# A convolution and pooling trunk on one core: modulation columns taken in twos, the layer norm's scaling in product order, and one pair of products halved around the mean

## The chip, the cores and the metric

One core of a Trainium2 chip runs the whole kernel in one launch. The metric is device time in microseconds (us): the median of several executions of the kernel. A single execution is also recorded by the hardware profiler; its rows are what is read here as "the profile" and "the trace". TensorE (PE) does the matmuls, and PEld is its weight load, which runs beside them. VectorE (DVE), ScalarE (ACT) and GpSimd (POOL) do the elementwise work, and SyncE (SP) issues most of the DMAs from memory.

## What is computed

```python
D_MODEL = 1024; SEQ = 1024; DEPTH = 2; CONV_WIDTH = 31; D_FF = 2816

def conformer_conv(h, w1, b1, w_dw, b_dw, ln_g, ln_b, w2, b2):
    u = h @ w1 + b1
    a, g = jnp.split(u, 2, axis=-1)
    u = a * jax.nn.sigmoid(g)
    u = causal_depthwise_conv(u, w_dw) + b_dw          # 31 taps
    u = jax.nn.silu(layer_norm(u, ln_g, ln_b))
    return u @ w2 + b2
...
c_act = jax.nn.silu(c)
for i in range(DEPTH):
    mod = c_act @ ada_w[i] + ada_b[i]
    sh_m, sc_m, g_m, sh_f, sc_f, g_f = jnp.split(mod, 6, axis=-1)
    h = modulate(rms_norm(x, norm_mix_g[i]), sh_m, sc_m)
    y = conformer_conv(h, ...) if i % 2 == 0 else multiscale_pool(h, ...)
    x = x + (1.0 + g_m)[:, None, :] * y
    h = modulate(rms_norm(x, norm_ffn_g[i]), sh_f, sc_f)
    y = (jax.nn.silu(h @ w_gate) * (h @ w_up)) @ w_down
    x = x + (1.0 + g_f)[:, None, :] * y
return rms_norm(x, final_g)
```

The inputs are float32. The six parts of `mod` (numbered j = 0 to 5) depend on the conditioning vector `c` alone. Here only layer 0 matters, the one with the convolution.

## The kernel before

**Tiling.** The 1024 positions are two chunks of 512, A and B. Channels lie on the 128 partitions, so an activation of a chunk is eight tiles (k = 0 to 7) of 128 x 512. Every weight and every activation of a large product is split into a high and a low part (`whi`, `wlo`, `hhi`, `hlo`, `vhi`, `vlo`), and `products` (L414) makes three matmuls of 512 columns of them, high by high, low by high and high by low, for each of the eight k. So one output tile of 128 channels takes 24 matmuls. All matmuls are recorded at one line (L128), and all elementwise operations at one line (L106), so in the rows one goes by tile names.

**Order.** The order of PE's instructions is that in which the program writes them. The other engines' queues are ordered by a scheduler from what each instruction depends on. Around the main products the program steps through `Task`s, generators that write side work. `pace` is called in the loops over `products` and steps them by a model clock: a task says `yield "load"`, and is not stepped again until the model clock has moved by the number that `LOAD` gives for that word. `finish` steps a task to its end at once. A chain of dependencies can be added by hand (`tc.add_manual_dep`).

**Layer 0.** Conv pairs: for each p of 8, `conv_in` makes an `a` tile and a `g` tile (24 products each) and `conv_glu` turns them into `u`, with a sigmoid on ACT and a multiply on DVE. The taps of the depthwise convolution run on DVE, ACT and POOL. A's pairs come first, then B's, with A's layer norm (`layer_norm_silu`) beside B's pairs. That norm sums the eight filtered tiles on DVE (`acc`), has PE form the mean (`mean`), subtracts, squares, has PE form the variance (`var`, one column for each 128 positions), computes a reciprocal root in a dozen small DVE steps, and has PE spread it over the partitions (`rstd`). Then each tile is scaled by `rstd` on DVE, passes through silu on ACT, and is split into `vhi` and `vlo`. The scheduler chooses the order of these scalings and splits. `conv_out` multiplies the eight tiles by the second weight (`y`, 8 output tiles, 192 products), ACT evicts (`t<-y`), and DVE adds to `x`. Squares of the new `x` give the next norm (`norm_a`, again a `var` and a `rstd`) behind which the first FFN's `gate` products start.

**Modulation columns.** Parts j = 0 and 1 are computed at the start of the kernel. Parts 2 to 5 come from `ada_columns` (L358) as a `Task` beside the conv pairs. For each j and each k it loads a tile `adaw` of 512 KB (128 x 1024, `ada_load`, L138, on SP's queue) and makes four matmuls of 256 columns (`ada`, counted x8 in the trace). That is 32 column steps. `adaw` has `ADA_BUFS` = 2 buffers. A load is written when the column two before it has been written, so it waits for that column on PE. After the eighth k of a j, `columns_done` copies the row off PSUM on ACT (`t<-ada`), turns it into columns by two small matmuls (`adac`), and adds the bias. When the flag `held` is set (before the last of B's pairs), the parts j = 3 to 5 that end after it keep their row in `held_back`, and `conv_out` writes their `columns_done` in its second step. `finish(T["ada", 0])` forces what columns are left.

**Weights.** `load_weight` loads a raw tile on SP, copies its high part on ACT, and makes the low part either by a subtraction or, with `summed`, by a negated copy on ACT followed by an accumulating DMA on POOL's queue (L408).

**End of this stretch.** The units are written in this order: B's pairs but the last, `held`, the finish of the columns, the finish of A's taps, B's last pair but for those `HOLD` = 1 holds, `need("ln_a")`, `conv_out(A)`, the task `norm_a`, the held pair, `need("norm_a")`, and then the first FFN.

Of the kernel before, what the change touches and what calls it, by code (L numbers as in the profile page):

```python
# [19 lines left out]
KT = D // P  # L20
# [26 lines left out]
PHTAPS = 29  # L47
PHLEN = 135
OUT_B = 3
LOAD = {"load": 2.5, "slow": 18.0, "next": 4.0}  # L50
AHEAD = 4
STRETCH = 1.35
LATER = 300
# [58 lines left out]
def trunk(ctx, tc, xT, c, vec, ada, adan, w1, w2, wgu, wdn, wpl, wph, out):  # L112
# [37 lines left out]
    def either(n):  # L150

        now = clock["PE"]
        v, g = (max(clock[e], now) + engines[e].price("tensor_tensor", n) for e in "VG")
        return V_ if v <= g else G_
# [29 lines left out]
    def pace(ahead=AHEAD):  # L184

        for t in [t for t in tasks if t.urgent or getattr(t, "free", False)]:
            while step(t, "V"):
                pass
        moved = True
        while moved and tasks:  # L190
            moved = False
            for e in "VG":
                if clock[e] < clock["PE"] + ahead:
                    moved = any(step(t, e) for t in list(tasks)) or moved
# [41 lines left out]
    def slot(ch, name, dt=F32R):  # L236

        return slots.tile([P, ch.n], dt, tag=f"s{ch.i}", name=nm(name))
# [5 lines left out]
    def bank(name):  # L244
        return ps.tile([P, 512], F32, tag="mm", name=nm(name))

    def spare_bank(name):

        return ps.tile([P, 512], F32, tag="ca", name=nm(name), bufs=2)
# [11 lines left out]
    def temp(n, name="t", bufs=0):  # L261
        t = tmp.tile([P, TMPW], F32, tag=name if bufs else "t", name=nm(name), bufs=bufs or 4)
        return t[:, :n]
# [47 lines left out]
    def ada_load(src):  # L311
        w = raws.tile([P, D], F32, tag="ada", name=nm("adaw"), bufs=ADA_BUFS)
        sync.dma_start(w, src)
        return w
# [43 lines left out]
    def ada_columns(js):  # L358


        todo = [(j, k) for j in js for k in range(KT)]
        src = lambda j, k: adan[k, :, (j - 2) * D : (j - 1) * D]
        ws = [ada_load(src(*t)) for t in todo[:ADA_BUFS]]
        for i, (j, k) in enumerate(todo):
            yield "load"
            if k == 0:
                acc = bank("ada")
            w = ws.pop(0)
            for g in range(4):
                matmul(acc[32 * g : 32 * g + 32, :Q], ccols[:, k, :], w[:, g * Q : g * Q + Q], start=k == 0, stop=k == KT - 1)  # L370
            clock["PE"] -= 1.3
            if i + ADA_BUFS < len(todo):
                ws.append(ada_load(src(*todo[i + ADA_BUFS])))
            if k == KT - 1 and (j == 2 or not held[0]):
                yield from columns_done(j, acc)
            elif k == KT - 1:
                held_back.append((j, acc))
# [36 lines left out]
    def products(out, wt, k, act, first, last, o=0, n=None):  # L414

        wk = slice(k * P, (k + 1) * P)
        for i, (wp, a) in enumerate(((0, 0), (0, 1), (1, 0))):
            cols = act[a][:, o : o + n] if n else act[a]
            matmul(out, wt[wp][:, wk], cols, start=first and i == 0, stop=last and i == 2)
# [149 lines left out]
    def conv_u(ch, p):  # L569
        u = st["u", ch.i, p] = wslot(ch, "u")  # L570
        if ch.i == 0:
            G_.memset(u[:, :HALO], 0.0)
        else:
            G_.tensor_copy(u[:, :HALO], uhalo[:, p, :])
        return u
# [9 lines left out]
    def conv_in(*todo):  # L585

        def emit(take):
            got = {}
            for each in todo:
                if each is None:  # L590
                    finish(T["norm_b"])
                    continue
                if callable(each):
                    each()
                    continue
                ch, p = each
                conv_u(ch, p)
                wts = got.setdefault(p, [])
                b = [bank("a"), bank("g")]
                for i in range(2):  # L600
                    if len(wts) == i:
                        wts.append(take())
                    for k in range(KT):
                        products(b[i], wts[i], k, st["h", ch.i][k], k == 0, k == KT - 1)
                        if k % 4 == 3:
                            pace()
                conv_glu(ch, p, *b)
                if ch.i == 0 and p not in PHASED:
                    T["taps", 0, p] = Taps(A, p)
        tiles = list(dict.fromkeys(e[1] for e in todo if isinstance(e, tuple)))  # L610
        unit(emit, *[w1[p, i] for p in tiles for i in range(2)])

    class Taps:


# [110 lines left out]
    def centred(vs, mean, n):  # L726
# [7 lines left out]
                V_.tensor_tensor(vs[k], vs[k], mean, op=SUB)  # L734
        yield

    def layer_norm_silu(ch):

        n = ch.n
        vs = [st["u", ch.i, k][:, HALO:] for k in range(KT)]  # L740
        acc = temp(n, "acc", 2)
        for k in range(1, KT):
            while not (st["taps", ch.i][k - 1] and st["taps", ch.i][k]):
                yield "wait"
            V_.tensor_tensor(acc, vs[0] if k == 1 else acc, vs[k], op=ADD)
            yield
        yield "stats"
        b = bank("mean")
        matmul(b, ones, acc, start=True, stop=True)
        if ch.i == 0:  # L750
            yield from centred(vs, b, n)
        else:
            for k in range(KT):
                V_.tensor_tensor(vs[k], vs[k], b, op=SUB)
                yield
        acc = yield from sum_sq([vs[k] for k in CENTRED], n)
        rstd = yield from mean_rsqrt(acc, n)
        S_.activation(tmp.tile([P, 16], F32, tag="col0", name=nm("col"), bufs=1)[:, 0:1], acc[:, 0:1], AF.Silu)
        hv = [(slot(ch, "vhi"), slot(ch, "vlo")) for _ in range(KT)]
        for k in range(KT):  # L760
            V_.tensor_tensor(vs[k], vs[k], rstd, op=MUL)
            sw = temp(n)
            S_.activation(sw, vs[k], AF.Silu, bias=V("conv_ln_b", k), scale=V("conv_ln_g", k))
            hi, lo = hv[k]
            if ch.i == 0 and k % 2 == 0:
                V_.tensor_copy(hi, sw)
            else:
                S_.copy(hi, sw)
            (either(n) if ch.i else (G_, V_)[k % 2]).tensor_tensor(lo, sw, hi.bitcast(F32), op=SUB)
            yield  # L770
        st["v", ch.i] = hv

# [517 lines left out]
    def need(*names):  # L1290
        unit(lambda take: finish(*(T[n] for n in names)))
# [44 lines left out]
    unit(lambda take: finish(*(T["taps", 0, p] for p in range(KT) if p not in PHASED)))  # L1336
    for p in rest[len(rest) - HOLD - HOLD_LN : len(rest) - HOLD]:
        conv_in((B, p))
    need("ln_a")
    sq_a = Squares(A)  # L1340
    conv_out(A, sq_a, lambda take: [now(columns_done(*g)) for g in held_back])
    unit(lambda take: T.__setitem__("norm_a", Task(norm(A, 0, True, ("h", 0), squares=sq_a), True)))
    for p in rest[len(rest) - HOLD :]:
        conv_in((B, p))
    need("norm_a")
    unit(lambda take: stretch.__setitem__(0, STRETCH))

# [135 lines left out]
```

## Time and profile before

| | us |
|---|---|
| median of 3 runs | 1840.85 (1838.78 to 1842.66) |
| profiled execution | 1842.04 |
| its span | 1840.2 |
| PE busy | 1777.9 (97%) |
| DVE busy | 1312.9 (71%) |
| ACT busy | 1040.9 (57%) |
| POOL busy | 588.4 (32%) |

The profiled execution's time is 1.8 us longer than the span of its instructions and 1.2 us above the median. Times of rows are counted from the span's start. In the rows of a view "[1.86 <-DMA x]" says that the engine stood idle for 1.86 us ahead and what ended the wait. Shares of busy time are averages over stages with different limits, so the change has to be read in the stretch that it touches: the conv layer of chunk A, up to about 323 us.

### The profile page before, as it was taken

Reading aid. Unit: us, or ns where it says so; the run is one execution under the profiler, and the core shown is the slowest. Engines: PE = TensorE matmul, PEld = TensorE weight load, DVE = VectorE, ACT = ScalarE, POOL = GpSimd, SP = SyncE. Lnnn points to the kernel's source line nnn. Section 1 sums busy time; section 2 is a strip of 40 time slices with the busy share of each in tenths; the row PEclk is TensorE's granted clock in tenths of the full one; section 3 lists DMA queues with packets and bytes.
Section 4 is the critical chain, followed back from the end, with each engine's and each line's share of the span. In section 5 each row is a group of like instructions: output and inputs, shape, how many; then the busy total and the mean of one; then the engine's idle time right before and its main releaser. Section 6 shows DMA issues by size and latency. Waiting matters only on the chain.

```text
span 1840.2 us, 26108 instructions
## 1 busy us (share of the span) xinstructions
PE 1777.9 (97%) x9672; PEld 1514.0 (82%) x9672; DVE 1312.9 (71%) x2125; ACT 1040.9 (57%) x1610; POOL 588.4 (32%) x628
## 2 busy tenths in 40 slices
PE   6999989999999999999999999999999999999996
PEld 4766677888888887889997888999988789999985
DVE  7789855988875238779978448778684468887735
ACT  3656666776647455555546456555564546555543
POOL 3479732877833111311116121111151211011111
PEclk9999999999999999999999999999999999999998
DMA  7978858888888987867766887655568866655562
GB/s 253 298 221 239 218 130 202 213 230 206 230 208 210 234 222 179 242 192 202 206 178 150 199 181 171 163 137 136 147 143 210 187 151 170 182 139 138 127 138 69
DMA packets 115953, 342.73 MB, mean 186 GB/s; under 512 B 11505, under 2 KB 21873, under 8 KB 115826
## 3 DMA queue, kind: packets, MB, share of 16 engines
q1 hardware_dynamic: 76944, 223.60, 36.7%
q0 software_dynamic: 37728, 116.41, 35.2%
q8 instruction: 76, 1.25, 0.3%
q10 hardware_dynamic: 1154, 1.05, 0.2%
q14 instruction: 51, 0.42, 0.1%
HBM read 336.83 MB, written 4.19 MB: 185 GB/s over the span
## 4 chain that ended last, share of the span: by engine, by line
PE 82%; DMA 6%; DVE 6%; ACT 2%; issue 2%; POOL 1%; SPq 0%; DVEq 0%; ACTq 0%; POOLq 0%
PE dn L128 22%; PE gate L128 22%; PE up L128 22%; PE y L128 6%; PE a L128 3%; PE g L128 3%; PE first L128 2%; DMA adaw<-in_adan_dram 2%; DMA raw<-in_wgu_dram 2%; DMA w<-in_wdn_dram 1%; DVE x L106 1%; DVE t L106 1%; DMA w<-in_wgu_dram 1%; ACT w L106 1%; PE ada L128 1%
## 5 line engine op out<-in xcount | busy, mean ns | idle before, releaser
L128 PE MATMUL dn<-ghi,w 128*128 128x512 f32 (+1 forms) x1440 | 470.0, 389 | 4.1 <-DMA w<-in_wdn_dram 2.7
L106 ACT ACTIVATE w<-raw 128x1024 fp32r<-128x1024 f32 (+1 forms) x262 | 243.0, 927 | 326.1 <-PE dn L128 99.0
L106 ACT CAST w<-raw 128x512 fp32r<-128x512 f32 (+1 forms) x392 | 322.1, 824 | 144.9 <-PE up L128 53.5
L106 DVE SCALAR_TENSOR_TENSOR x<-dn,gains,x 128x512 f32<-128x512 f32 (+1 forms) x360 | 263.3, 736 | 83.2 <-PE dn L128 80.4
L128 PE MATMUL gate<-hhi,w 128*128 128x512 f32 (+1 forms) x1088 | 313.0, 361 | 4.2 <-DMA w<-in_wgu_dram 3.9
L128 PEld LDWEIGHTS dn<-ghi,w 128*128 128x128 f32 x1440 | 269.1, 188 | 57.8 <-DMA w<-in_wdn_dram 3.6
L128 PE MATMUL up<-hhi,w 128*128 128x512 f32 (+1 forms) x1088 | 310.1, 358 | 0.0
L128 PE MATMUL dn<-glo,w 128*128 128x512 f32 (+1 forms) x720 | 279.2, 388 | 0.9 <-POOL glo L106 0.9
L106 POOL TENSOR_TENSOR pa<-pa,pr 128x512 f32<-128x512 f32 x168 | 229.7, 1419 | 22.5 <-ACT pr L106 19.5
L128 PEld LDWEIGHTS gate<-hhi,w 128*128 128x128 f32 x1088 | 198.2, 190 | 36.6 <-DMA w<-in_wgu_dram 4.7
L1008 POOL DMA_DIRECT2D w<-in_wgu_dram x80 | 69.6, 871 | 495.8 <-ACT w L106 161.7
L128 PEld LDWEIGHTS up<-hhi,w 128*128 128x128 f32 x1088 | 196.6, 189 | 30.5
L128 PE MATMUL gate<-hlo,w 128*128 128x512 f32 (+1 forms) x544 | 196.1, 361 | 1.5 <-DVE hlo L106 1.5
L128 PE MATMUL up<-hlo,w 128*128 128x512 f32 (+1 forms) x544 | 194.6, 358 | 0.0
L408 POOL DMA_DIRECT2D w<-in_wgu_dram x96 | 86.2, 898 | 324.8 <-ACT w L106 301.1
L106 DVE TENSOR_TENSOR t<-t,up 128x512 f32<-128x512 f32 (+1 forms) x88 | 55.0, 625 | 169.3 <-PE up L128 156.6
L106 DVE SCALAR_TENSOR_TENSOR ca<-u,vecs,ca 128x512 f32<-128x512 f32 x252 | 174.1, 749 | 0.7
L128 PEld LDWEIGHTS dn<-glo,w 128*128 128x128 f32 x720 | 136.2, 189 | 24.0 <-POOL glo L106 1.2
L106 ACT ACTIVATE pr<-u,vecs 128x512 f32<-128x512 f32 x168 | 113.3, 715 | 16.7 <-POOL pa L106 6.9
L128 PEld LDWEIGHTS gate<-hlo,w 128*128 128x128 f32 x544 | 103.7, 191 | 18.2 <-DVE hlo L106 2.3
L128 PEld LDWEIGHTS up<-hlo,w 128*128 128x128 f32 x544 | 102.7, 189 | 15.5
L106 DVE TENSOR_TENSOR w<-raw,w 128x512 fp32r<-128x512 f32 (+1 forms) x122 | 84.4, 700 | 31.0 <-ACT w L106 27.9
(188 smaller groups left out, 3385.5 us busy)
## 6 DMA issues: line engine op xcount, KB each, us to landing
raw<-in_wgu_dram SPq DMA_DIRECT2D x176, 512.0 KB, 5.2
w<-in_wgu_dram POOLq DMA_DIRECT2D x96, 512.0 KB, 8.2
raw<-in_wdn_dram SPq DMA_DIRECT2D x88, 512.0 KB, 5.5
adaw<-in_ada_dram SPq DMA_DIRECT2D x64, 512.0 KB, 5.8
w<-in_wdn_dram POOLq DMA_DIRECT2D x48, 512.0 KB, 8.3
raw<-in_w_dram SPq DMA_DIRECT2D x44, 512.0 KB, 6.0
w<-in_wgu_dram POOLq DMA_DIRECT2D x80, 256.0 KB, 5.4
w<-in_w_dram POOLq DMA_DIRECT2D x34, 512.0 KB, 8.3
```

What stands on the lines that cost most here:

```text
L106: self.last = self.order(getattr(self.eng, name)(out, *args, **kw))
L128: last_mm[0] = nc.tensor.matmul(out, lhsT, rhs, start=start, stop=stop, **kw).ins.name
L408: order(nc.gpsimd.dma_start(as_src(lo), src, accum_op=ADD))
L1008: order(nc.gpsimd.dma_start(lo, src, accum_op=ADD))
```

## The change

It has three parts.

1. The columns are taken in twos. `ada_columns` yields "load" ahead of every second column only, with 7.0 on the model clock instead of 2.5, and "late" (14.0) ahead of the first. The loads are issued in twos when a pair is written, instead of one for each column.
2. The scaling, silu and splits of chunk A's layer norm are written by `silu_in_order`. It chains DVE's multiplies, casts and subtractions by hand in the order in which the products take the tiles, with the multiply two tiles ahead. The even tiles' high part is cast on DVE and the odd ones' on ACT. The odd tiles and tile 0 are subtracted on DVE and the other even ones on POOL. (Before, DVE subtracted the odd tiles, and POOL all even ones.)
3. `conv_halves` splits B's held pair. Its `a` half is written ahead of `need("ln_a")`. Its `g` half and the `conv_glu` stay behind `conv_out`.

```diff
-LOAD = {"load": 2.5, "slow": 18.0, "next": 4.0}
+LOAD = {"load": 7.0, "late": 14.0, "slow": 18.0, "next": 4.0}
...
         for i, (j, k) in enumerate(todo):
-            yield "load"
+            if i % ADA_BUFS == 0:
+                yield "load" if i else "late"
...
-            if i + ADA_BUFS < len(todo):
-                ws.append(ada_load(src(*todo[i + ADA_BUFS])))
+            if i % ADA_BUFS == ADA_BUFS - 1:
+                ws += [ada_load(src(*t)) for t in todo[i + 1 : i + 1 + ADA_BUFS]]
...
+    def conv_halves(ch, p):
+        got = {}
+        def first(take):
+            conv_u(ch, p)
+            got["a"] = spare_bank("a")
+            wt = take()
+            for k in range(KT):
+                products(got["a"], wt, k, st["h", ch.i][k], k == 0, k == KT - 1)
+                if k % 2:
+                    pace()
+        def second(take):
+            b, wt = bank("g"), take()
+            for k in range(KT):
+                products(b, wt, k, st["h", ch.i][k], k == 0, k == KT - 1)
+                if k % 2:
+                    pace()
+            conv_glu(ch, p, got["a"], b)
+        return (first, w1[p, 0]), (second, w1[p, 1])
...
+    def silu_in_order(vs, rstd, hv, n):
+        last = [None]
+        def chained():
+            if last[0] is not None:
+                tc.add_manual_dep(V_.last.ins, last[0], edge, reason="as the products take them")
+            last[0] = V_.last.ins.name
+        def scaled(k):
+            V_.tensor_tensor(vs[k], vs[k], rstd, op=MUL)
+            chained()
+            sw = temp(n)
+            S_.activation(sw, vs[k], AF.Silu, bias=V("conv_ln_b", k), scale=V("conv_ln_g", k))
+            return sw
+        ahead = [scaled(0), scaled(1)]
+        for k in range(KT):
+            sw = ahead.pop(0)
+            hi, lo = hv[k]
+            if k % 2 == 0:
+                V_.tensor_copy(hi, sw)
+                chained()
+            else:
+                S_.copy(hi, sw)
+            if k % 2 or k == 0:
+                V_.tensor_tensor(lo, sw, hi.bitcast(F32), op=SUB)
+                chained()
+            else:
+                G_.tensor_tensor(lo, sw, hi.bitcast(F32), op=SUB)
+            if k + 2 < KT:
+                ahead.append(scaled(k + 2))
+            yield
...
         hv = [(slot(ch, "vhi"), slot(ch, "vlo")) for _ in range(KT)]
+        if ch.i == 0:
+            yield from silu_in_order(vs, rstd, hv, n)
+            st["v", ch.i] = hv
+            return
         for k in range(KT):
...
             hi, lo = hv[k]
-            if ch.i == 0 and k % 2 == 0:
-                V_.tensor_copy(hi, sw)
-            else:
-                S_.copy(hi, sw)
-            (either(n) if ch.i else (G_, V_)[k % 2]).tensor_tensor(lo, sw, hi.bitcast(F32), op=SUB)
+            S_.copy(hi, sw)
+            either(n).tensor_tensor(lo, sw, hi.bitcast(F32), op=SUB)
...
+    held_a, held_g = conv_halves(B, rest[-1])
+    unit(*held_a)
     need("ln_a")
     sq_a = Squares(A)
     conv_out(A, sq_a, lambda take: [now(columns_done(*g)) for g in held_back])
     unit(lambda take: T.__setitem__("norm_a", Task(norm(A, 0, True, ("h", 0), squares=sq_a), True)))
-    for p in rest[len(rest) - HOLD :]:
-        conv_in((B, p))
+    unit(*held_g)
     need("norm_a")
```

What this does to the queues is seen at four places. In the rows a name is "out<-inputs" with the number of the buffer, and x4 or x2 says how many instructions a row stands for.

First, PE's queue around chunk A's `rstd`. Before, the last `g` products of the pair ahead stand in front of it (its `var` stands 13 rows higher), and the `y` products right behind:

```order
L128 MATMUL g_2127<-hhi_718,w_2016 128x512
L128 MATMUL g_2127<-hlo_719,w_2016 128x512
L128 MATMUL g_2127<-hhi_718,w_2017 128x512
L128 MATMUL rstd_2201<-ident,col_2177 128x128 x4
L128 MATMUL y_2281<-vhi_2208,w_2119 128x512
L128 MATMUL y_2281<-vlo_2209,w_2119 128x512
```

Now the same `rstd` has `var` and eight columns right in front, and the `a` products of the held half behind it:

```order
L128 MATMUL var_2131<-ones,acc_2033 128x1 x4
L128 MATMUL ada_2149<-adaw_2015,ccols 32x256 x4
L128 MATMUL ada_2149<-adaw_2017,ccols 32x256 x4
L128 MATMUL ada_2149<-adaw_2158,ccols 32x256 x4
L128 MATMUL ada_2149<-adaw_2160,ccols 32x256 x4
L128 MATMUL ada_2149<-adaw_2187,ccols 32x256 x4
L128 MATMUL ada_2149<-adaw_2189,ccols 32x256 x4
L128 MATMUL ada_2149<-adaw_2199,ccols 32x256 x4
L128 MATMUL ada_2149<-adaw_2201,ccols 32x256 x4
L128 MATMUL rstd_2211<-ident,col_2137 128x128 x4
L128 MATMUL a_2276<-hhi_688,w_2046 128x512
L128 MATMUL a_2276<-hlo_689,w_2046 128x512
```

The last eight columns (all of j = 5) moved from among the products to between `var` and `rstd`, and 24 `a` products moved between `rstd` and the first `y`.

Second, SP's queue of loads at that place. Before, column loads and the raw weight tiles alternate, and the columns end before `raw_2267`:

```order
L138 DMA adaw_1826<-in_adan_dram 128x1024
L138 DMA adaw_1855<-in_adan_dram 128x1024
L403 DMA raw_2128<-in_w_dram 128x1024
L138 DMA adaw_1910<-in_adan_dram 128x1024
L138 DMA adaw_1929<-in_adan_dram 128x1024
L403 DMA raw_2267<-in_w_dram 128x1024
L403 DMA raw_2274<-in_w_dram 128x1024
L403 DMA raw_2342<-in_w_dram 128x1024
```

Now the last six column loads stand in a row:

```order
L138 DMA adaw_2017<-in_adan_dram 128x1024
L404 DMA raw_2383<-in_w_dram 128x1024
L404 DMA raw_2421<-in_w_dram 128x1024
L138 DMA adaw_2158<-in_adan_dram 128x1024
L138 DMA adaw_2160<-in_adan_dram 128x1024
L138 DMA adaw_2187<-in_adan_dram 128x1024
L138 DMA adaw_2189<-in_adan_dram 128x1024
L138 DMA adaw_2199<-in_adan_dram 128x1024
L138 DMA adaw_2201<-in_adan_dram 128x1024
L404 DMA raw_2459<-in_w_dram 128x1024
```

Each of the six waits for the column that used its buffer, and `raw_2459` and all later weight loads wait behind them in the queue.

Third, PE's queue inside `y`. `adac` of the held part j = 5 stands behind the first 48 of the 192 products (before, no `adac` stands there):

```order
L128 MATMUL y_2309<-vhi_2232,w_2167 128x512
L128 MATMUL y_2309<-vlo_2233,w_2167 128x512
L128 MATMUL y_2309<-vhi_2232,w_2168 128x512
L128 MATMUL adac_2378<-quarters,t_2376 128x4 x2
L128 MATMUL y_2390<-vhi_2218,w_2174 128x512
L128 MATMUL y_2390<-vlo_2219,w_2174 128x512
```

The products of the next two output tiles, `y_2390` and its neighbour, now stand behind this `adac`.

Fourth, the ACT queue that feeds it. Before, at the same place it holds the evictions of the first two `y` tiles, weight copies, and the first two squares:

```order
L106 ACTIVATE t_2331<-y_2281,vecs 128x512
L106 CAST w_2351<-raw_2349 128x1024
L106 ACTIVATE w_2352<-raw_2349 128x1024
L106 ACTIVATE t_2336<-y_2282,vecs 128x512
L106 CAST w_2389<-raw_2387 128x1024
L106 ACTIVATE acc_2334<-x_0_77 128x512
L106 ACTIVATE t_2339<-x_1_78 128x512
L106 ACTIVATE w_2390<-raw_2387 128x1024
L106 ACTIVATE t_2381<-y_2356,vecs 128x512
```

Now the copy of the column row, `t_2376<-ada_2149`, stands among them:

```order
L106 ACTIVATE t_2358<-y_2308,vecs 128x512
L106 CAST w_2385<-raw_2383 128x1024
L106 ACTIVATE w_2386<-raw_2383 128x1024
L106 ACTIVATE t_2363<-y_2309,vecs 128x512
L106 CAST w_2423<-raw_2421 128x1024
L106 ACTIVATE acc_2361<-x_0_77 128x512
L106 ACTIVATE t_2366<-x_1_78 128x512
L106 COPY t_2376<-ada_2149 128x256
L106 ACTIVATE w_2424<-raw_2421 128x1024
```

The copy stands behind both evictions and both squares, and `adac_2378` reads what it writes.

At the start of the stretch PE's column steps stood singly behind every 12 products from row 209 of its queue. Now the first pair stands at row 269, behind 72 products, and further pairs follow at rows 308, 347, 385 and so on to the twelfth at 714, two rows ahead of the mean.

## The prediction

> **What bounds the kernel now.** I read the page first, then TensorE's waits, then the chain of waits, then the busy time by stretches.
>
> ```profile
> PE 1777.9 (97%) x9672; PEld 1514.0 (82%) x9672; DVE 1312.9 (71%) x2125; ACT 1040.9 (57%) x1610; POOL 588.4 (32%) x628
> ```
>
> TensorE (PE) has a matmul in flight 97% of the span (1840.2 us), so the time is the length of its stream plus the places where it stands still or runs cold. Behind the first gate products of the first FFN (at 323.18 us) PE's queue is row for row the same in both kernels. I therefore sum over 72.1 to 323.18 only and take the rest as shifted. The cuts below are chosen where PE reaches the mean, the variance, the end of `rstd`, the first `y` products, the end of `y`, the end of the second `rstd`, and the first full run of gate products. Columns: length, then busy time of PE, weight loads, DVE, ACT, POOL, then granted clock, DMA share, GB/s.
>
> ```profile
> 72.10:228.77 156.67, 148.92 (x884) 104.99 (x884) 132.09 (x198) 103.90 (x147) 125.19 (x119) 0.98 0.83 234
> 228.77:240.72 11.95, 11.95 (x54) 9.55 (x52) 8.52 (x13) 10.09 (x15) 4.97 (x5) 1.00 0.77 166
> 240.72:245.24 4.52, 4.51 (x27) 3.84 (x27) 2.01 (x12) 1.84 (x4) 0.00 (x0) 1.00 0.77 186
> 245.24:252.28 7.04, 0.80 (x1) 0.29 (x1) 7.02 (x11) 4.26 (x7) 2.54 (x2) 0.77 0.77 166
> 252.28:297.55 45.27, 45.27 (x192) 37.33 (x193) 13.29 (x20) 28.33 (x38) 10.00 (x10) 0.96 0.68 155
> 297.55:307.51 9.96, 9.96 (x53) 8.51 (x53) 3.45 (x14) 4.91 (x6) 2.47 (x3) 1.00 0.90 204
> 307.51:323.18 15.67, 14.21 (x61) 11.10 (x61) 15.64 (x23) 12.56 (x18) 6.37 (x6) 1.00 0.64 165
> ```
>
> Two stretches hold idle or slow PE time: the first, with clock 0.98, and the gap 245.24 to 252.28. The waits of PE from 70 to 330 us (total, times, longest) say why:
>
> ```profile
> PE ada L128 <- DMA adaw<-in_adan_dram: 7.8, 5, 3.1
> PE y L128 <- DVE vhi L106: 5.3, 1, 5.3
> PE y L128 <- POOL vlo L106: 1.0, 1, 1.0
> ```
>
> The prices come from the chain (start, length, what):
>
> ```profile
> 95.51 1.08 PE ada L128 x8
> 96.59 4.01 PE a L128 x12
> 100.61 0.57 PE ada L128 x8
> 101.18 2.95 PE g L128 x12
> ...
> 115.10 1.00 PE rstd L128 x8
> ...
> 225.76 0.34 PE adac L128 x4
> ...
> 232.56 5.44 PE a L128 x24
> 238.00 2.72 PE g L128 x12
> ```
>
> and from PE's own order of time, where a wait of 1.86 us is followed by a slow stretch:
>
> ```profile
> 83.71 0.64 PE L128 MATMUL ada<-adaw,ccols 128*32 128x256 f32 x8 [1.86 <-DMA adaw<-in_adan_dram]
> 88.81 0.64 PE L128 MATMUL ada<-adaw,ccols 128*32 128x256 f32 x8
> ```
>
> A product of 512 columns takes 5.44/24 = 0.2267 us. A modulation column (`ada`) takes 0.57, and the twelve products behind it 2.95 instead of 2.72, so a column alone costs 0.80 and two in a row 0.57 × 2 + 0.23 = 1.37. Cold, a column takes 1.08 and the twelve products 4.01: 1.57 us lost. From 83.71 to 88.81 pass 5.10 us, where column and twelve products are worth 3.52: 1.58 lost again.
>
> **The change, first stretch (columns in twos).** Before the mean the old order has 32 columns, the new one 24, in twelve pairs; 12 more products and two fewer `adac` (0.34, with what they cost the product behind, in the ratio of the column's 0.80 to 0.57, some 0.45 each) stand there. Working: 156.67 − (32 × 0.80 − 12 × 1.37 = 9.2) − 7.8 of waits − 3.1 cold − 0.9 + 12 × 0.2267 = 138.4 if nothing waits, a gain of 18.3. Three things can give some of it back.
>
> First, weights. With no columns ahead of it, the third product of pair 5's first half, the first to use a low part made by an accumulating load (`w_604`), comes at 72.1 + 50 × 0.2267 = 83.4. Before, that load was issued and landed so:
>
> ```profile
> L408 POOL DMA_DIRECT2D w<-in_w_dram x1: 1040/1040/1040, 78.3 to 78.3; - x1
> DMA to landing us min/median/max: 10.2/10.2/10.2
> ```
>
> That is 88.5. In the new order ACT does two squares and one tap product more before it, about 1.2 us, and POOL one more add, so I put the issue at 77.3; with 10.2 it lands at 87.5, a wait of 4.0 and 1.6 cold: +5.6. Bounds: with the 5.8 of the fastest such load (its row stands below) 0; with the issue at 78.3 as before, 6.7. I take the 10.2, since it is the same load.
>
> Second, the column loads. Both of a pair are now issued when the pair before is done and needed 36 products, 8.2 us, later.
>
> ```profile
> DMA to landing us min/median/max: 3.5/4.8/11.1
> DMA to landing us min/median/max: 5.8/9.5/13.3
> ```
>
> The first row is the 30 column loads: median 4.8, worst 11.1. Two at once land somewhat later than one; I allow one or two late pairs, +1.5 (0 to 5).
>
> Third, DVE, whose sum of the eight filtered tiles the mean needs:
>
> ```profile
> 133.00:229.00 96.00, 93.21 (x589) 66.54 (x585) 87.18 (x123) 60.53 (x86) 81.97 (x79) 1.00 0.85 234
> 227.00 1.42 DVE L106 TENSOR_TENSOR acc<-acc,u 128x512 f32<-128x512 f32 x2
> ```
>
> The sum was ready at 228.4, just ahead of PE at 228.77: nearly a second bound. DVE's taps and POOL's are as many as before (POOL 78 adds in both). From the end of chunk B's splits at 133, DVE has 87.2 us of work in 95.4. Those splits start behind a `rstd` that PE reaches at 72.1 + 120 × 0.2267 + 2 × 1.37 + 1 = 103.0, plus 5.6 = 108.6, against 115.1 before; so DVE ends 6.5 earlier, and up to 8.2 more if none of its waits recurs: 213.7 to 221.9. PE's sum gives 72.1 + 138.4 + 5.6 + 1.5 = 217.6. I take 217.6: −11.2 (ends −18.3 and −4.5, the second with DVE's late end and a late pair on top).
>
> **Mean to variance.** The same 48 products and one `adac`: +0.45.
>
> **Variance to `rstd`: the columns left over.** The slower pace leaves the last four pairs (j = 5) to the forced finish; they stand in one run between `var` and `rstd`. There are two buffers, so pairs two to four are issued only when the column before in the same buffer is done: three round trips through memory with nothing else on PE, and `rstd`, the scaling and all of `y` queued behind. On SP the six loads stand ahead of weights that are wanted some 45 us later, which costs nothing. Per buffer a round is landing plus a cold column: the first beside weight loads, 5.5 + 1.1, two in a quiet queue at 3.9 + 1.1 (loads in the quiet stretch before took this):
>
> ```profile
> DMA to landing us min/median/max: 3.6/3.6/4.0
> ```
>
> 0.79 (`var`) + 1.37 + 16.6 + 0.4 (other buffer) + 0.9 (`rstd`) = 20.0 against 4.52: +15.5. Ends: landing 3.5 and warm columns, 16.3, +11.8; one landing of 11.1 and two of 6, 26, +21.5. The rsqrt chain and the scaling's table load lie beside this at no cost.
>
> **`rstd` to the end of `y`: the held half.** The 24 products of B's last pair now fill the gap: 5.44 + 1.57 cold = 7.0. They cover the scaling in its new order. Its parts took, by groups (name, shape, count, busy time and mean ns, then idle time ahead):
>
> ```profile
> L106 DVE TENSOR_TENSOR u<-u,rstd 128x512 f32<-128x512 f32 x8 | 4.9, 683 | 1.3 <-PE rstd L128 1.3
> L106 ACT ACTIVATE t<-u,vecs 128x512 f32<-128x512 f32 x8 | 6.1, 805 | 2.8 <-POOL vlo L106 2.8
> L106 POOL TENSOR_TENSOR vlo<-t,vhi 128x512 fp32r<-128x512 f32 x4 | 5.6, 1390 | 7.1 <-DVE vhi L106 6.1 <-issue 1.0
> ```
>
> DVE's chain is now 8 multiplies, 4 casts and 5 subtractions of this size, 17 × 0.7 = 11.9, and a first wait for table load and silu of 0.68 + 1.28 + 0.80 − 2 × 0.68 = 1.4. So the last low part is ready at 13.3, and PE, at 1.36 a tile behind the 7.0, wants it at 16.5. The tightest tile is the seventh: its cast ends at 12.6, POOL's subtraction at 14.0, PE comes at 15.2. So the waits of 5.3 and 1.0 go, with about 1 to spare. Without that cover the tail of splits would cost up to 1.5. Then 192 × 0.2267 = 43.5. But inside `y`, behind the first 48 products, stands `adac` of the held columns, and its row copy is in ACT's queue behind both evictions, three weight copies and the squares of `x_0` and `x_1`. Before, those ran so:
>
> ```profile
> 265.01 0.67 ACT L106 ACTIVATE t<-y,vecs 128x512 f32<-128x512 f32 x1
> 269.51 0.62 ACT L106 ACTIVATE t<-x 128x512 f32<-128x512 f32 x1
> 221.23 0.36 ACT L106 COPY t<-ada 128x256 f32<-128x256 f32 x1
> ```
>
> The first 48 ended at 297.55 − 144 × 0.2267 = 264.9, the second square at 270.1; with the copy (0.36) PE waits 5.6, then 0.35 for `adac` and 1.57 cold. Together 7.0 + 43.5 + 7.5 = 58.0, against 7.04 + 45.27 = 52.3: +5.7 (+2.6 with no cold stretch, +6.5 with the tail uncovered).
>
> **`y` to the first gate run.** 18 products, `var`, 6 products, `rstd` instead of 24, `var`, 12, `rstd`, 12. DVE's rsqrt took 303.81 to 306.19, so `rstd` ends 8.3 behind `y`, not 9.96. But B's last half (`g`) now ends only here; its sigmoid needs a table load and stands ahead of the splits on DVE, which start at about 9.9, as before.
>
> ```profile
> 303.81 0.17 DVE L106 TENSOR_SCALAR var<-var 128x4 f32<-128x4 f32 x1 [2.62 <-PE var L128]
> 306.03 0.16 DVE L106 SCALAR_TENSOR_TENSOR col<-var,col 128x4 f32<-128x4 f32 x1
> 307.54 2.72 DVE L106 SCALAR_TENSOR_TENSOR t<-x,gains,rstd 128x512 f32<-128x512 f32 x4 [1.35 <-PE rstd L128]
> 320.91 0.79 DVE L106 SCALAR_TENSOR_TENSOR hlo<-t,mod,hhi 128x512 fp32r<-128x512 f32 x1
> 239.98 1.28 ACT L106 ACT_TABLE_LOAD   x1
> 241.28 0.20 ACT L106 ACTIVATE col<-acc 128x1 f32<-128x1 f32 x1
> ```
>
> From 307.54 to 321.6 DVE did 20 operations; now 17, about −2.0, and nearly 3 us of idle PE cools it. 25.63 becomes 23.7: −1.9 (0 to −3). The table load there took 1.28, 1.30 to the start of the function behind. The Trainium skill (ScalarE: Activation LUTs, What ACT_TABLE_LOAD costs) gives a switch as a load of about 1283 ns and a drain of about 1380. By that this stretch would come to −0.5 and the sum to +10; the row shows the 1.28 and no drain, and the row decides.
>
> **Sum.** −11.2 + 0.45 + 15.5 + 5.7 − 1.9 = +8.6. The profiled execution took 1842.04, 1.2 above the median of 1840.85; put on the median this is 1849.4.
>
> **Rivals.** *Short landings.* If loads land as fast as the quietest here, the weight comes in time, no pair is late, the mean is reached at 210.5 and the four pairs take 16.3: −18.3 + 0.45 + 11.8 + 5.7 − 1.9 = −2.3, 1838.6: no measurable change, since 0.2%, 3.7 us, is about what a measurement here can tell from none. For it: 3.6 in a quiet stretch. Against it: the DMA share of 0.83 in the first stretch. It decides for faster only below 3.0 us a landing, as each microsecond counts three times; none of the 30 was under 3.5. The Trainium skill (DMA: Bandwidth & Descriptors, Anatomy of one DMA) fits 2.0 us plus bytes over 436e3, for 512 KB an estimate of 3.2; by that this rival ends at 1837.7. The trace's shortest, 3.5, comes near it and the median does not.
>
> *Slow landings, or DVE last.* If loads of two keep landing as in the crowded first stretch, the four pairs take 26: +21.5 in place of 15.5, 1855.4. DVE's late end instead gives 1856. For it: the worst of 11.1 and 13.3 there. Against it: no weight load can overtake SP's six.
>
> *No wait in `y`.* If the copy ran ahead of the evictions, 7.2 would go: 1842.2. ACT is in order, so I give this nearly nothing.
>
> **How the numbers follow.** Forecast (1845 to 1853) 0.62, slow rival 0.15, both slower by over 0.2%; short landings 0.20, split into 0.14 of no change and 0.06 of faster; no wait in `y` 0.03, no change. So faster 0.06, same 0.17, slower 0.77. The range leaves the outer halves of the rivals out: 1841 to 1857.
>
> **What would show it.** PE waits on `adaw` early nearly gone but some 15 us of them between `var` and `rstd`; a wait of PE `a` on the weight's DMA near 83; a wait of `adac` on ACT of 5 to 6 inside `y`; no wait on `vhi`; the mean near 217. I am wrong if the four pairs take under 14 us, if the mean comes before 210, or if PE waits again behind 323.

## The result, and the profile after

The changed kernel takes 1864.26 us (median of 4 runs, 1862.75 to 1865.73) against 1840.47 for the kernel before in the same session. The ratio is 1.0131 with a 95% interval of 1.0116 to 1.0147, so it is 23.8 us slower. The profiled execution took 1862.75 with a span of 1861.0, which is 20.8 longer than the span before.

The cuts of the prediction (mean, variance, end of `rstd`, end of `y`, first full run of gate products) fall here in the changed kernel. The columns are as before: length, busy time of PE, weight loads, DVE, ACT and POOL, granted clock, DMA share, GB/s.

```profile
72.10:218.97 146.87, 136.84 (x821) 104.78 (x819) 137.16 (x195) 104.25 (x146) 125.58 (x117) 0.98 0.82 231
218.97:234.15 15.18, 15.18 (x57) 11.73 (x57) 8.60 (x14) 9.33 (x15) 5.39 (x6) 0.82 0.46 110
234.15:258.97 24.82, 10.29 (x82) 4.41 (x81) 2.66 (x13) 3.77 (x4) 0.88 (x1) 0.58 0.66 183
258.97:319.05 60.08, 54.55 (x221) 44.45 (x221) 19.40 (x31) 33.70 (x45) 11.20 (x12) 0.89 0.61 134
319.05:345.58 26.53, 21.45 (x90) 17.02 (x89) 20.73 (x40) 17.99 (x24) 9.26 (x9) 0.87 0.55 133
```

| stretch | before | after | measured | predicted |
|---|---|---|---|---|
| to the mean | 156.67 | 146.87 | −9.8 | −11.2 |
| mean to variance | 11.95 | 15.18 | +3.2 | +0.45 |
| variance to the end of `rstd` | 4.52 | 24.82 | +20.3 | +15.5 |
| `rstd` to the end of `y` | 52.31 | 60.08 | +7.8 | +5.7 |
| `y` to the first full gate run | 25.63 | 26.53 | +0.9 | −1.9 |
| sum | | | +22.4 | +8.6 |

The last cut, 345.58, is the old 323.18 moved by 22.4. That is how much later the first down products start, the next landmark behind it (367.18 against 344.78). The two profiled executions give 1.6 back after that. The granted clock stands out in these rows: 0.82, 0.58, 0.89 and 0.87 in stretches where it was 0.96 or more before, but for the 0.77 of the gap. The prediction charged slow columns between variance and `rstd`, and some 1.57 us of slow products at each of three places.

PE's waits in that stretch (total, times, longest) and parts of the chain (start, length, what) show the places:

```profile
PE ada L128 <- DMA adaw<-in_adan_dram: 15.9, 7, 8.1
PE mean L128 <- DVE acc L106: 7.5, 1, 7.5
PE adac L128 <- ACT t L106: 6.4, 2, 5.5
PE gate L128 <- ACT hhi L106: 2.9, 1, 2.9
PE gate L128 <- DVE hlo L106: 1.1, 1, 1.1
PE rstd L128 <- DVE col L106: 1.1, 1, 1.1
PE a L128 <- DMA w<-in_w_dram: 0.3, 1, 0.3
```

```profile
218.97 2.07 PE mean L128 x2
221.05 4.44 PE a L128 x12
...
236.00 9.54 DMA adaw<-in_adan_dram
246.72 4.33 DMA adaw<-in_adan_dram
252.24 3.60 DMA adaw<-in_adan_dram
256.96 2.01 PE rstd L128 x8
...
282.41 1.01 PE adac L128 x4
283.42 35.63 PE y L128 x144
```

Two of the prediction's waits stand there at the forecast size: `adaw` between variance and `rstd` (8.06 + 0.49 + 2.03 + 1.33 + 1.36 + 1.27 = 14.5 of the 15.9), and `adac` inside `y` at 5.5. No wait on `vhi` is left. The wait of `mean` on DVE, 7.5, and that of `gate` on `hhi`, 2.9, are new.

### The profile page after: what moved, and what is told of

The parts are those of the page before. It is cut to its first block, busy times and chain, and to the rows that moved or that the text cites. A ratio compares the mean times of both kernels' runs of the same rounds, so it can differ in the third digit from the quotient of the medians.

```text
span 1861.0 us, 26111 instructions
## 1 busy us (share of the span) xinstructions
PE 1779.7 (96%) x9672; PEld 1519.9 (82%) x9672; DVE 1321.0 (71%) x2125; ACT 1047.3 (56%) x1616; POOL 590.4 (32%) x628
## 3 DMA queue, kind: packets, MB, share of 16 engines
q10 hardware_dynamic: 1154, 1.05, 0.2%
## 4 chain that ended last, share of the span: by engine, by line
PE 79%; DVE 7%; DMA 6%; issue 3%; ACT 3%; POOL 2%; SPq 0%; DVEq 0%; POOLq 0%; ACTq 0%
PE dn L128 22%; PE up L128 21%; PE gate L128 21%; PE y L128 6%; PE a L128 2%; PE first L128 2%; PE g L128 2%; DMA adaw<-in_adan_dram 2%; DMA w<-in_wgu_dram 1%; ACT w L106 1%; POOL pa L106 1%; DMA w<-in_wdn_dram 1%; DVE ca L106 1%; DVE t L106 1%; DVE x L106 1%
## 5 line engine op out<-in xcount | busy, mean ns | idle before, releaser
L106 POOL TENSOR_TENSOR pa<-pa,pr 128x512 f32<-128x512 f32 x172 | 239.3, 1481 | 27.6 <-ACT pr L106 24.3
```

Source lines behind the costliest of these rows:

```text
L106: self.last = self.order(getattr(self.eng, name)(out, *args, **kw))
```

## Experiments

Every ratio is against the kernel before in the same session, whose median was 1840.15, 1841.18, 1839.36 and 1838.97 us in the four sessions. "The landmark" below is the start of the first down products: 344.78 before, 367.18 after.

**Which part makes the loss.** The parts were run apart: part 1 alone on the kernel before, parts 2 and 3 without part 1, part 3 alone, and part 2 alone.

```diff
# part 1 alone, on the kernel before
-LOAD = {"load": 2.5, "slow": 18.0, "next": 4.0}
+LOAD = {"load": 7.0, "late": 14.0, "slow": 18.0, "next": 4.0}
# and the lines of ada_columns as in the change; nothing else
# parts 2 and 3: the changed kernel with these lines as before
# part 3 alone: conv_halves and its three units; part 2 alone: silu_in_order and its call
```

> The kernel before with part 1 alone (columns in twos at 7.0 and 14.0). Theory: the mean near 219, 15 to var, 25 to the end of rstd (eight columns with round trips), the gap of 7 ahead of y as before, y with the wait of adac of some 5 and a cold stretch, and 25.6 behind: the gate run near 343 to 345, 1859 to 1863, so part 1 alone makes the whole loss. Rival (the held a half, which runs cold behind the columns, shares in it): under 1855.

> Columns singly and paced as before (part 1 undone), the scaling in order and the halved pair kept. Theory: the mean as before near 228.8, var to rstd 4.5, rstd to the end of y 49 (24 products more, but no wait on vhi), then about 26.5 to the gate run: 320.8 against 323.2, 1837 to 1840. Rival (the halved pair is what costs, by its waits of gate on hhi and hlo): over 1845.

> The kernel before with part 3 alone (the halved pair), columns and scaling as before. Theory: the 24 products cover the gap ahead of y whatever order DVE takes, so the same as with the scaling in order, within 1 us: 1837 to 1841. Rival (the scheduler's order of the scaling leaves late tiles): waits of y on vhi or vlo of 2 to 5 us behind the a half, 1840 to 1845.

> The kernel before with part 2 alone (the scaling and splits in the order of the products), columns as before and the held pair whole behind y. Theory (the gap of 7.0 ahead of y shrinks to the 3.7 to 4.2 that the first split needs behind rstd, and the later tiles keep up with PE at 1.36 a tile): 2 to 3 off, 1837 to 1839, and the same size of gain as the halved pair alone gives, since both fill the same gap. Rival (without products to cover it the tail of the splits makes PE wait tile by tile): the gap at the first tile goes down, but waits on vhi and vlo of 2 to 3 in sum come behind it, 1840 to 1842.

| run | median us | ratio, 95% interval | landmark |
|---|---|---|---|
| part 1 alone | 1862.51 | 1.0113 (1.0093 to 1.0132) | 369.15 |
| parts 2 and 3 | 1838.96 | 0.9986 (0.9973 to 0.9999) | 345.28 |
| part 3 alone | 1837.61 | 0.9986 (0.9972 to 1.0000) | 343.27 |
| part 2 alone | 1836.25 | 0.9987 (0.9974 to 1.0000) | 342.50 |

All four times came out as their theories had them, part 2 alone a little lower. Part 1 alone makes the loss. Parts 2 and 3 each bring about 2.5 us, at the edge of what can be told from none, and together no more than either. Both fill the gap ahead of `y`, which would explain that. PE's waits behind the first `rstd` show the gap, first with part 3 alone, then with part 2 alone, then with both:

```profile
PE gate L128 <- ACT hhi L106: 1.6, 1, 1.6
PE gate L128 <- DVE hlo L106: 1.3, 1, 1.3
PE rstd L128 <- DVE col L106: 1.1, 1, 1.1
PE y L128 <- POOL vlo L106: 0.9, 1, 0.9
PE y L128 <- DVE vlo L106: 0.2, 1, 0.2
```

```profile
PE y L128 <- DVE vhi L106: 2.1, 1, 2.1
PE gate L128 <- DVE hlo L106: 1.5, 2, 1.0
PE y L128 <- DVE vlo L106: 0.5, 2, 0.3
```

```profile
PE gate L128 <- ACT hhi L106: 1.6, 1, 1.6
PE gate L128 <- DVE hlo L106: 1.4, 1, 1.4
PE rstd L128 <- DVE col L106: 1.1, 1, 1.1
PE y L128 <- DVE vlo L106: 0.4, 1, 0.4
PE y L128 <- ACT vhi L106: 0.2, 1, 0.2
```

Before, `y` waited 5.3 and 1.0, and `gate` 1.5 behind it. With products in the gap the waits of `y` fall to 1.1, and to 0.6 with the scaling ordered by hand as well. With the order alone they fall to 2.6. But with part 3 fewer products are left behind `y`: `rstd` then waits 1.1, and `gate` 2.9 or 3.0 instead of 1.5. Part of the gap moved from one end of `y` to the other.

**The eight columns between variance and `rstd`.** Here the six loads of the last three pairs are left out, and PE's queue stays as it is.

```diff
-                ws += [ada_load(src(*t)) for t in todo[i + 1 : i + 1 + ADA_BUFS]]
+                ws += [ada_load(src(*t)) for t in todo[i + 1 : i + 1 + ADA_BUFS]] if i < 24 else []
...
             w = ws.pop(0)
+            if i >= 24:
+                ws.append(w)
```

> The changed kernel, in which the last three pairs of columns multiply the two tiles of the first of the four again, so their six loads are left out (part j = 5 is computed from the wrong weights); every PE instruction stays where it was. Theory (var to the end of rstd takes 24.8 because each pair waits for its loads): no wait of ada on adaw there, eight columns of about 0.57 run beside the root, 6 to 8 us instead of 24.8, the following products warm: 17 to 19 off, 1844 to 1847. Rival (another wait, the root on DVE or a late weight, stands behind the loads and takes their place): 10 us off or less, over 1853.

It measured 1846.66, ratio 1.0029 (1.0016 to 1.0041), against 1.0131 of the changed kernel: 1.0% or some 19 us less. PE's own order of time:

```profile
235.69 3.66 PE L128 MATMUL ada<-adaw,ccols 128*32 128x256 f32 x64
240.16 1.16 PE L128 MATMUL rstd<-ident,col 128*128 128x128 f32 x8 [0.81 <-DVE col L106]
```

The eight columns now run in 3.66 us, half a microsecond each, and `rstd` ends 6.3 behind the start of `var` instead of 24.8. The theory holds: what costs there is the loads' round trips, with the slow clock that they bring (1.08 for a column between them, 0.46 here), and not the columns' own work. The 7.5 at the mean and the 5.5 at `adac` are unchanged in this run, and it is still slower than before.

**A quicker pace.** With the pace 5.0 all 16 pairs stand ahead of the mean.

```diff
-LOAD = {"load": 7.0, "late": 14.0, "slow": 18.0, "next": 4.0}
+LOAD = {"load": 5.0, "late": 5.0, "slow": 18.0, "next": 4.0}
```

> The changed kernel with two numbers of the pace set back: "load" 5.0 for 7.0 and "late" 5.0 for 14.0. All 32 columns, still in twos, then stand ahead of the mean; none stands between var and rstd and no adac in y. Theory (the loss is the eight columns left over, 24.8 us from var to the end of rstd, the cold stretch behind the mean's wait, and the 5.5 us wait of adac in y): var to rstd back to about 4.5, rstd to the end of y about 49, the mean near 219 as in the changed kernel because DVE's sum sets it: the gate run near 312, 1829 to 1833. Rival one (columns in twos cost PE waits wherever they stand): waits of ada on adaw of over 8 us ahead of the mean, 1838 to 1845. Rival two (the loss is the halved pair and the gate products behind it): it stays above 1850.

It measured 1840.95, ratio 1.0006 (0.9991 to 1.0021): the loss is gone, but not the 8 to 12 us more that the theory gave. Rival one is what happened. PE's waits, and the landing of the column loads ahead of the mean:

```profile
PE ada L128 <- DMA adaw<-in_adan_dram: 16.7, 9, 4.3
DMA to landing us min/median/max: 3.6/6.1/12.4
```

Nine waits of 16.7 us in all put the mean at 233.9, later than the 228.77 before and not near 219 as the theory had it. Between two pairs stand 24 products, 5.4 us, and half of the loads take 6.1 or longer. So two buffers carry neither pace: at 5.0 the pairs wait early, and at 7.0 the last four are left over.

**`adac` inside `y`.** The held part's copy and `adac` are moved behind all of `y`.

```diff
-            if then is not None and len(ds) > 1:
+            if then is not None and ds == (KT - 1,):
                 unit(then)
```

> The changed kernel with the held part's columns_done behind all of y instead of behind the first 48 products. Theory (adac waits for a copy that stands behind both evictions and two squares on ACT, and the pause cools PE): the wait of 5.5 and the cold stretch of about 1.6 go, with no new wait behind y if the copy is done by then: 6 to 7 us off, 1856 to 1858. Rival (the wait moves to the end of y, where again two squares and an eviction stand ahead of the copy): 0 to 3 off, 1861 to 1864.

It measured 1860.48, ratio 1.0114 (1.0095 to 1.0133), and the landmark is at 366.54. The wait moved with it, at 3.2 of the 5.5:

```profile
315.42 1.02 PE L128 MATMUL adac<-quarters,t 128*128 128x4 f32 x4 [3.22 <-ACT t L106]
```

The rival was right in kind: at the end of `y` the copy again has the last eviction and square ahead of it on ACT. The time lies between the two forecasts, and the intervals of this run and the changed kernel overlap, so no gain is shown.

**The columns left over go inside `y`, paced.**

```diff
-    unit(lambda take: held.__setitem__(0, True))
-    unit(lambda take: finish(T["ada", 0]))
...
-    conv_out(A, sq_a, lambda take: [now(columns_done(*g)) for g in held_back])
+    conv_out(A, sq_a)
+    unit(lambda take: finish(T["ada", 0]))
```

> The changed kernel without the forced finish of the columns ahead of y: the four pairs left over are paced on among the products (one behind var, three in y), and the finish stands behind y. Theory: their loads land beside products, so var to the end of rstd takes 7 to 9 (one pair and 12 products), y grows by three pairs (4.1) and an adac, the mean stays near 219 (DVE's sum, 7.5 of wait): the gate run near 317 to 319, 1834 to 1838. Rival (loads in y land late, since the weight loads of y and of the FFN fill the queue): waits of ada in y of over 5 us, 1840 to 1845.

It measured 1837.44, ratio 0.9986 (0.9974 to 0.9998), and the landmark is at 342.52. No column in `y` waited:

```profile
236.42 1.07 PE L128 MATMUL ada<-adaw,ccols 128*32 128x256 f32 x16
247.55 1.07 PE L128 MATMUL ada<-adaw,ccols 128*32 128x256 f32 x16
257.90 1.07 PE L128 MATMUL ada<-adaw,ccols 128*32 128x256 f32 x16
271.37 1.07 PE L128 MATMUL ada<-adaw,ccols 128*32 128x256 f32 x16
277.98 0.50 PE L128 MATMUL adac<-quarters,t 128*128 128x4 f32 x4
```

So the four pairs that took 22 us of PE's time between variance and `rstd` cost about 1 each among products. This edit takes 27 us off the changed kernel by ratio (1.0131 to 0.9986). Leaving out the loads took some 19. The other 8 are near what the wait of 5.5 at `adac` and the slow clock behind it cost, since `adac` does not wait in `y` here. No run takes that part away alone. The wait of 7.5 at the mean is still there in this run, so it does not by itself make the loss.

**Further in that direction.** The first of these runs sets the pace to 5.5 and 10.0 in that kernel. The second also writes the halved pair's sigmoid and multiply behind the norm's scaling. The third does that at the slow pace.

```diff
# the first
+LOAD = {"load": 5.5, "late": 10.0, "slow": 18.0, "next": 4.0}
# the second and the third
-            conv_glu(ch, p, got["a"], b)
+            got["g"] = b
+
+        def third(take):
+            conv_glu(ch, p, got["a"], got["g"])
...
     unit(*held_g)
     need("norm_a")
+    unit(*held_u)
```

> The run with the columns in y (finish behind y), with "load" 5.5 and "late" 10.0 for 7.0 and 14.0: 13 pairs ahead of the mean instead of 12, one more before var, one behind var, one ahead of y. Theory (PE waits 7.5 for DVE's sum at the mean, so columns put there are free up to that): the mean stays at 219 to 221 with a wait of 3 to 5, y without pairs, 2 to 4 less than that run: 1833 to 1836. Rival (pairs every 30 products and fewer wait for their loads, as nine did for 16.7 us at a pace of 5.0): waits of ada on adaw of over 8 us, the mean at 223 or later, 1837 to 1842.

> That kernel (5.5, 10.0, finish behind y), with the sigmoid and multiply of the halved pair written behind the norm's scaling instead of ahead of it. Theory (the first gate products wait 2.9 for hhi because the sigmoid's table load and the multiply stand ahead of the scaling on ACT and DVE): that wait falls to under 1.5, 1.5 to 3 less than the run without it: 1831 to 1834. Rival (DVE's four first scalings in a row, 2.7, set the first hhi whatever stands ahead): the wait stays within 0.5 of what it was and the time within 1.

> The run with the columns in y at the slow pace (7.0, 14.0, finish behind y; 1837.4), with the halved pair's sigmoid and multiply written behind the norm's scaling. Theory (at a pace of 5.5 this cut the wait of gate on hhi from 2.9 to 1.7, and that is independent of the pace): the same 1.2 and some of the cold products behind it, so the first down products 1 to 2 earlier than the 342.5 of that run: 1835 to 1837.5, which a measurement here can hardly tell from 1837.4 but which would be below the kernel before with an interval clear of one. Rival (the wait is set by the four scalings in a row on DVE): no change in the wait, 1837 to 1839.

| run | median us | ratio, 95% interval | landmark |
|---|---|---|---|
| pace 5.5 | 1839.26 | 0.9991 (0.9980 to 1.0002) | 348.00 |
| pace 5.5, sigmoid later | 1839.54 | 0.9992 (0.9980 to 1.0003) | 345.95 |
| slow pace, sigmoid later | 1835.37 | 0.9988 (0.9974 to 1.0002) | 339.43 |

The pace of 5.5 gave its rival: waits on `adaw` of 8.9 us in five, and the mean at 228. The wait at the mean did go down from 7.5 to 1.7, but because PE came later. DVE's sum came later too, at 227.97 against 220.72 with the slow pace, so room for columns there was not free. The sigmoid's place is one cause of the wait of `gate` on `hhi`, which fell from 2.9 to 1.7 in both pairs of runs. That is not the forecast 1.5 or less, and the time did not move measurably: 1831 to 1834 was missed at the pace of 5.5, and at the slow pace 1835.37 lies in the forecast range, but its interval reaches past one.

**The held half cut smaller.** Part 3 alone, with 12 products ahead of `y` in place of 24.

```diff
-            for k in range(KT):
-                products(got["a"], wt, k, st["h", ch.i][k], k == 0, k == KT - 1)
+            for k in range(4):
+                products(got["a"], wt, k, st["h", ch.i][k], k == 0, False)
# the other four k stand at the start of second
```

> The kernel before with the held pair split otherwise: 12 products of its a half ahead of y, the other 12 and the g half behind. Against the run with the whole a half ahead (parts 2 and 1 undone, 1837.6): the 12 products cover 2.7 of the 3.7 to 4.2 that the first split needs, so y waits some 1 to 2 more; behind y 6 products stay behind rstd and cover 1.4 of the 3 that gate waits there, and rstd no longer waits 1.1 for the root. Theory (waits only move between the two ends): within 2 us of that run, 1836 to 1839. Rival (the wait ahead of y grows by the whole 2.7): 1840 or more.

It measured 1844.26, ratio 1.0023 (1.0009 to 1.0036). That is the rival's side: `y` waits 2.5 and 1.2 for the splits, 2.6 more in sum than with the whole half ahead. A wait of 1.1 on a weight is new here, and a slow stretch lies behind them.

## Why the prediction was wrong

The direction was right, and so were the two main causes, both of part 1: columns left over between variance and `rstd`, and `adac` waiting inside `y`. The size was not: +8.6 against +22.4 in the profile, and 1849.4, at most 1857, against 1864.3. All five terms of the sum came out dearer. Three steps failed. The first round of column loads was put at 6.6 us and took 10.7. The slow clock behind the added waits was charged too little, or at nothing behind the mean and ahead of `gate`, and cost about 8.5 us more than the sum had. And the last term took DVE's operations as its limit, where PE's products set the end. A fourth, the time of the mean, came near by luck.

*To the mean (−11.2, measured −9.8).* The size is near, but not for the reason given. The chain of the changed kernel has the weight's load:

```profile
76.72 6.13 DMA w<-in_w_dram
```

The weight `w_604` landed in 6.1 us instead of the 10.2 that I took from the old trace, so PE waited 0.3 and not 4.0 (0.7 to 2.7 in the other runs with columns in twos at a pace of 5.5 or slower). One pair was late by 1.3. PE was at the mean at 211.5 (218.97 less its wait of 7.5), at the early end of my range. DVE's sum was ready 7.5 later, at 218.97, inside the 213.7 to 221.9 that the text had. What failed here is "I take 217.6": it charged the delay to a weight and a late pair, when it was one wait at the mean. What keeps DVE so long is open, since no run changes its work there.

*Mean to variance (+0.45, measured +3.2).* I let the mean start warm, as it did before:

```profile
228.77 1.02 PE L128 MATMUL mean<-acc,ones 128*128 128x512 f32 x2
```

Behind a wait of 7.5 the mean took 2.07 instead of about 1, and the 12 products behind it 4.44 instead of 2.72. That is 2.8, the whole of the miss.

*Variance to `rstd` (+15.5, measured +20.3).* The mis-sized piece is the first round of loads, "the first beside weight loads, 5.5 + 1.1". Its landing took 9.54, and the round 10.7 with the column behind it. The other two landings took 4.33 and 3.60 where 3.9 was forecast. What was different shows in the last two columns (DMA share, GB/s) of the stretches around the first issue at 235.6:

```profile
225.00:230.00 5.00, 5.00 (x26) 4.15 (x25) 4.58 (x8) 4.08 (x7) 1.28 (x2) 1.00 0.00 0
230.00:235.00 5.00, 5.00 (x31) 4.28 (x33) 0.74 (x3) 3.06 (x4) 0.92 (x1) 1.00 0.83 165
235.00:240.00 5.00, 0.94 (x16) 0.28 (x12) 2.64 (x13) 2.92 (x4) 0.88 (x1) 0.82 0.95 239
240.00:246.00 6.00, 1.50 (x12) 0.41 (x16) 0.00 (x0) 0.00 (x0) 0.00 (x0) 0.50 0.70 190
```

From 225 to 230 nothing moves, and SP's next raw load waits until 229.62. At 235 everything comes at once: a raw weight, an accumulating load and two columns at 239 GB/s. That the loads land late because they come together fits these rows, but no run here tests it alone. The other 1.1 is a cold `rstd`, 2.01 against the 0.9 of the sum.

*`rstd` to the end of `y` (+5.7, measured +7.8).* The 24 products in 7.01 and the wait of 5.5 are as forecast. The 144 products behind `adac` took 35.63 and not 32.6 + 1.57, and `adac` itself 1.01 and not 0.35. PE stayed slow until 289.4, for 7.0 us, where 1.57 lost at about half speed stands for some 3 us. The trace before had a longer case that the price left out: behind the wait of 5.30 PE ran slow from 250.53 until about 255.9.

*`y` to gate (−1.9, measured +0.9).* I saw the sigmoid ahead of the splits, but counted fewer DVE operations as a gain. DVE did do fewer, 17. But that count limits the stretch only if its last split comes last. Before, it did:

```profile
321.76 0.50 PE L128 MATMUL gate<-hlo,w 128*128 128x512 f32 x1 [0.96 <-DVE hlo L106]
```

In the changed kernel PE waits for DVE no more after 332.4, and the products set the end. Ahead of that PE had too little else to do: `rstd` waited 1.1, `gate` 2.9 and 1.1, and the products behind ran cold, as PE's order of time has it (one product in 0.63 at half speed, in 0.39 at full):

```profile
330.51 0.79 PE L128 MATMUL gate<-hhi,w 128*128 128x512 f32 x1 [2.90 <-ACT hhi L106]
332.39 0.80 PE L128 MATMUL gate<-hlo,w 128*128 128x512 f32 x1 [1.09 <-DVE hlo L106]
332.99 0.63 PE L128 MATMUL gate<-hhi,w 128*128 128x512 f32 x1
...
336.40 0.63 PE L128 MATMUL up<-hlo,w 128*128 128x512 f32 x1
...
337.93 0.39 PE L128 MATMUL up<-hhi,w 128*128 128x512 f32 x1
```

The sigmoid is only part of that, since `gate` still waits 1.7 for the first `hhi` when it is moved away. The text said that idle PE cools here, and left it at about nothing in the sum; against the same products before, the slow clock cost some 2.5.

More than half of the 13.9 is thus the slow clock: 2.8 + 1.1 + 1.4 + 0.7 and some 2.5 in the first `gate` and `up` products, 8.5 in all. The range failed because it was made of one late piece at a time. Here a slow stretch followed each of the long waits, and they added up.

Of the rivals, *slow landings, or DVE last* was nearest, with 1855.4 and 1856. Its first half came nearly whole (+20.3 against +21.5). DVE was last at the mean too, but only 1.4 past the forecast instead of 6.7. The 26 of its first half is also added up wrongly: landings of 11.1, 6 and 6, three cold columns of 1.1 and the other terms of the sum (0.79 + 1.37 + 0.4 + 0.9) make 29.9, which is +25.3 and 1859.2. *Short landings* takes 3.2 us as an estimate from the Trainium skill (DMA: Bandwidth & Descriptors, Anatomy of one DMA). That section gives its fit for DMAs issued from GpSimd, and the column loads are issued from SP. Of the ten between 196 and 262 us none landed in under 3.6.

## What to carry to other kernels

Work that lies hidden among products costs what its loads' round trips cost when a forced finish puts it where PE has nothing else: eight columns that run in 3.7 us took 22. When a pace is slowed, count what is left over at the end and where the finish puts it, or let the work run on past that point. With a fixed number of buffers, spacing and left-over work are one trade, so two paces should be compared by both.

## What the runs showed of the hardware

The slow clock after a wait is dearer and less regular than the prediction's one price of 1.57 us. In PE's order of time of the run with part 2 alone, a wait of 2.15 is followed by products at full speed and only later by slow ones:

```profile
248.68 0.49 PE L128 MATMUL y<-vhi,w 128*128 128x512 f32 x1 [2.15 <-DVE vhi L106]
249.74 0.63 PE L128 MATMUL y<-vhi,w 128*128 128x512 f32 x2
250.60 1.05 PE L128 MATMUL y<-vhi,w 128*128 128x512 f32 x2
```

Two products in 0.63 are at full speed and in 1.05 at half. So the slow stretch begins between 1.1 and 1.9 us after the wait is over. Behind the wait of 5.53 in the changed kernel it lasted 7.0 us, and behind the longer one of 7.47 at the mean about 5.5, so its length does not follow the wait's. Among the last six columns the clock of 0.50 held from 240 to 258, with a wait of 0.5 to 2.0 us between one burst of 1.1 us and the next. The Trainium skill (TensorE: Matmul & The Clock Gate, Part 1: The HAM clock gate) has the clock halved after an idle window of about 3.4 us and restored after about as long of sustained work, judged in windows that run free of the kernel. The halved clock agrees with the rows, and a delay of this kind would fit windows that run free. The 2.15 does not agree with 3.4 as a threshold for a single wait, nor the 7.0 with 3.4 as a fixed length. Whether whole windows explain both, no run here tests.
